# Early adaLN vectors as TensorE products beside the weight slabs, filter parameters inside the first FFN, and layer norm sums accumulated ahead of TensorE

## The chip, the cores and the metric

The kernel runs on one core of one Trainium2 chip. The metric is the device time of one execution in microseconds. A core has a matrix engine (TensorE, PE in the profile, with its weight loads as PEld), three other engines that compute (VectorE as DVE, ScalarE as ACT, GpSimd as POOL), and SyncE (SP), which here only starts transfers. Each engine works through its own list of instructions in order. Transfers run on 16 DMA engines, through queues; an instruction on SP, or on POOL, puts a transfer into a queue.

## The reference

Two layers of a decoder trunk work on 512 tokens of 1024 features, all in float32. In both layers each sub-layer is an RMS norm whose result is scaled and shifted by vectors from a conditioning vector c, then a mixer, then an addition that a gate vector from c scales. Layer 0 has a Mamba-2 mixer and a dilated attention mixer in parallel, layer 1 a convolution module with a layer norm; each layer ends with a SwiGLU FFN.

```python
cs = jax.nn.silu(c)
mod = cs @ ada_w[i] + ada_b[i]               # [1024] @ [1024, 6144]
sh1, sc1, g1, sh2, sc2, g2 = split(mod, 6)   # 1024 values each
h = rms_norm(x, norm_mix_g[i]) * (1 + sc1) + sh1
x = x + g1 * mix
h = rms_norm(x, norm_ffn_g[i]) * (1 + sc2) + sh2
x = x + g2 * swiglu(h, wg, wu, wd)
```

The product for mod is the adaLN work. The 6144 values of a layer are 48 columns of 128: columns 0 to 7 are sh1, 8 to 15 sc1, 16 to 23 g1, 24 to 31 sh2, 32 to 39 sc2, 40 to 47 g2. The first two are wanted at the start, g1 with the first output chunk of the mixer, the others only in the FFN. The convolution module computes

```python
u = a * sigmoid(gt)                           # from h @ w1 + b1
u = causal_depthwise_conv(u, w_dw, b_dw)      # 31 taps per feature
mu = mean(u); var = mean((u - mu) ** 2)       # layer norm over 1024 features
u = silu((u - mu) * rsqrt(var + eps) * ln_g + ln_b)
out = u @ w2 + b2
```

## The kernel before

Activations lie with features on the 128 partitions and the 512 tokens along the row: a tensor of 1024 features is 8 tiles of 128 x 512. A large product is float32 made of three products of a faster type: weights and activations are split into a high and a low part, and high x high, low x high and high x low are summed (`products`, lines 221, 222 and 224). A weight slab (`slab`) is 1 MB: it is loaded by SP into a buffer with the tag `raw`, of which the pool `wpool` has two, then ACT casts the high part in two halves (L208) and DVE subtracts for the low part (L209). TensorE writes its results into banks of PSUM, which have tags too: `pj`, `A`, `B` and `C`, with two banks each. Whatever wants a bank or a buffer of a tag waits until an earlier user has been read.

The program is written in the order of the stages below; a planner, which reckons with the time of each instruction, puts them into the list of each engine, the earlier written ones first where several could go. `issue_after` holds an instruction back until a named one.

1. Start (to about 44 us): adaLN columns 0 to 15 with `ada_wide` (eight multiply-adds per 4 columns on DVE, then four transposes on PE and a sum on DVE), the first norm, and the time steps dt of the SSM.
2. SSM (to about 345 us): four groups. `ssm_inputs(g)` makes ten outputs from five slabs: B and C of the group (`bc`), four tiles `x`, four tiles `z`. `ssm_group(g)` goes through four chunks of 128 tokens: `ar` is loaded from DRAM, ACT does relu and exp (L507, L508), PE does `px`, `pb`, `pd`, `po` and `pst`, the last two carrying the state from chunk to chunk; `pst` is in bank C. In the program `ssm_group(g)` stands ahead of `ssm_inputs(g + 1)`, and behind groups 0 and 1 stands `ada_rows` for columns 16 to 19 and 20 to 23: eight loads of 256 KB on SP into three buffers of their own, a matmul for each with silu(c) as a weight of 32 columns (`cs32`, of which only the first isn't zero), the four column tiles of PE in turn, then four sums over the partitions as matmuls with one column (`adac`, L176). Results are in bank C.
3. Attention (345 to about 800 us): for each of eight pairs of heads `att_pair` (scores, exp, three transposes `pt` into bank C for each of two heads, weights of the branches sent through DRAM as `w_dram`, and the results `at`, `ath`, `atl`), then `ada_some`, then `att_inputs` of the next pair (slabs `wa`, `wb`, and `wv` in every second). `ada_some` does three `ada_pool` jobs: a load of 512 KB on POOL's queue into one buffer, four POOL instructions (L184, L186), a PE transpose in bank C (L153) and a sum on DVE, for one column each; the eight calls make columns 24 to 47. Output chunks stand behind some pairs (`y_chunk`, `mixed_chunk`); the last, `mixed_chunk(3)`, is done in two halves of tokens, with the sums of the next norm (`Norm` n1) in it.
4. Parameters of layer 1: `rows` loads vectors as rows and transposes them. The 31 taps become `taps`, then 16 DVE copies make `wcol` (L921), and `filters(0)` to `filters(3)` make the convolution weights on POOL (L930).
5. FFN of layer 0 (to about 1255 us): `Norm.finish` (L285 to L325), slabs, products. `side` is called behind each of its gate and up slabs and does the layer 1 adaLN columns with `ada_wide`, four at a time.
6. Convolution module (to about 1490 us): `conv(k, cols)` for eight tiles k, each in one or two halves of the tokens; `layer_norm(c)` for each half; `pw2`. In `layer_norm` the mean comes from eight matmuls with a constant weight of 1/1024 (`mu`, L1011), DVE subtracts it, ACT squares, and the variance comes from 16 matmuls with one column (`var`, L1021). A float32 matmul of this kind is two instructions in the profile.
7. FFN of layer 1, the last norm, the output.

Of the kernel before, what the change touches and what calls it, by code (L numbers as in the profile page):

```python
# [9 lines left out]
F32 = mybir.dt.float32  # L10
# [3 lines left out]
ALU = mybir.AluOpType  # L14
# [63 lines left out]
def trunk_kernel(ctx: ExitStack, tc, a, out, dbg=None):  # L78
# [86 lines left out]
    def ada_rows(pool, l, j0):  # L165

        ps = bank("C", f"adar{l}_{j0}")
        for k in range(KT):
            w = pool.tile([P, 512], F32, tag="adaw", name=f"adaw{l}_{j0}_{k}", bufs=3)
            nc.sync.dma_start(w, a["ada_w"][l][k * P:(k + 1) * P, j0 * P:j0 * P + 512])  # L170
            PE.matmul(ps[k % 4 * 32:(k % 4 + 1) * 32, :], cs32[:, k, :], w, start=k < 4, stop=k >= 4)
# [3 lines left out]
        for j in range(4):  # L175
            PE.matmul(pm[:, j:j + 1], rw[:, j * P:(j + 1) * P], ones[:, 0:1], start=True, stop=True)  # L176
        V.tensor_tensor(mod[l][:, j0:j0 + 4], pm, adab[l][:, j0:j0 + 4], op=ALU.add)

    def ada_pool(pool, bufs, l, j):
        w = pool.tile([P, 1024], F32, tag="adaw", name=f"adap{l}_{j}", bufs=bufs)  # L180
        G.dma_start(w.rearrange("p (k c) -> p k c", k=KT),
                          a["ada_w"][l][:, j * P:(j + 1) * P].rearrange("(k p) c -> p k c", p=P))
        w3 = w.rearrange("p (k c) -> p k c", k=KT)
        G.tensor_tensor(w3, w3, cs.unsqueeze(2).broadcast_to([P, KT, P]), op=ALU.mult)  # L184
        for n in (512, 256, 128):
            G.tensor_tensor(w[:, 0:n], w[:, 0:n], w[:, n:2 * n], op=ALU.add)  # L186
        ada_finish(l, w, j, 1)

    def ada_jobs(l, lo, hi):
        return [(l, j) for j in range(lo, hi)]  # L190
# [299 lines left out]
    cs32 = ssm.tile([P, KT, 32], F32, name="cs32", bufs=1)  # L490
# [66 lines left out]
    jobs = [(0, j) for j in range(24, 48)]  # L557

    def ada_some(pool, bufs, n):
        for _ in range(min(n, len(jobs))):  # L560
            ada_pool(pool, bufs, *jobs.pop(0))

# [348 lines left out]
    taps = const.tile([P, 31 * KT], F32, name="taps")  # L911
    rows([(dwr[0:128], 128)], "dw0", taps[:, 0:128])
    rows([(dwr[128:248], 120)], "dw1", taps[:, 128:248])

    wcol = const.tile([P, KT, 4, 8], F32, name="wcol")
    V.memset(wcol[96:128, :, :, 7], 0.0)
    taps3 = taps.rearrange("p (t k) -> p k t", k=KT)
    for sft in range(4):
        for g in range(4):
            o = wcol[sft * 32:(sft + 1) * 32, :, g, 0:8 if sft < 3 else 7]  # L920
            V.tensor_copy(o, taps3[g * 32:(g + 1) * 32, :, sft:TAPS:4])  # L921
# [4 lines left out]
    w4 = {}  # L926

# [5 lines left out]
    for k in range(4):  # L933
        filters(k)
# [22 lines left out]
    with tc.tile_pool(name="conf", bufs=2) as conf:  # L957
        h = nxt.finish(const, g_mix1, mod[1][:, 0:8], XG)
        w1 = a["cv_w_pw1"][0]
        cv, u4 = {}, {}  # L960
# [8 lines left out]
        def conv(k, cols):  # L969
# [36 lines left out]
        def layer_norm(c):  # L1006
# [3 lines left out]
            for i, k in enumerate(range(KT)):  # L1010
                PE.matmul(mb, meanw, cv[k, n], start=i == 0, stop=i == KT - 1)  # L1011
            vp = bank("C", f"var{n}", (P, nb))
            for i, k in enumerate(range(KT)):
                t = cv[k, n]
                V.tensor_tensor(t, t, mb, op=ALU.subtract)
                if i % 2 == 0:
                    two = tmp.tile([P, T], F32, tag="st_sq", name=f"cvq{k}_{n}")
                sq = two[:, i % 2 * w:(i % 2 + 1) * w]
                S.activation(sq, t, AF.Square)
                for b in range(nb):  # L1020
                    PE.matmul(vp[:, b:b + 1], sq[:, b * P:(b + 1) * P], ones[:, 0:1], start=i == 0 and b == 0,  # L1021
                              stop=i == KT - 1 and b == nb - 1)
# [86 lines left out]
```

## Time and profile before

| what | value |
|---|---|
| time, median of 3 runs | 1847.52 us (1847.27 to 1849.47) |
| the profiled execution | 1844.22 us, of which the span is 1842.5 us |
| PE busy | 1764.2 us, 96% of the span |
| DVE, ACT, POOL busy | 999.3, 740.7, 347.6 us |
| bytes moved | 247.85 MB, mean 135 GB/s |

The span is the time from the first to the last recorded instruction; the profiled execution's time is 1.7 us more. A row of the timeline gives the start, the time it took, the engine, the line of the program, the operation, the tile that it writes and those it reads, and in square brackets how long its engine had been idle and what it waited for; "x4" means that so many like instructions stand in the row. A row of waits names who waited, for whom, the total, how many times, and the longest. Busy times of PE are modelled for the ends of matmuls, which are pipelined, so neighbours overlap and the time from one start to the next is what counts. PEclk is the clock that the throttle granted to TensorE, as a share of full speed.

### The profile page before, as it was taken

What the parts mean: (1) busy time and instruction counts of PE and PEld (TensorE: products, weight loads), DVE (VectorE), ACT (ScalarE), POOL (GpSimd) and SP (SyncE); (2) the same over time, 40 slices, a digit from 0 to 9 for tenths busy, and PEclk for the clock granted to TensorE, in tenths of its full rate; (3) what the DMA queues carried; (4) which work ended last, traced back from release to release, by engine and by line L of the source; (5) the groups of instructions that cost most, each with busy time, mean ns of one, the idle gap of its engine ahead of it and who ended that gap; (6) DMA issues with size and microseconds to landing.
All of it is one profiled execution on the core that took longest, in us unless ns stands there. A gap on an engine that the chain in (4) does not pass through costs nothing.

```text
span 1842.5 us, 25006 instructions
## 1 busy us (share of the span) xinstructions
PE 1764.2 (96%) x9775; PEld 1438.8 (78%) x9775; DVE 999.3 (54%) x1944; ACT 740.7 (40%) x1473; POOL 347.6 (19%) x278
## 2 busy tenths in 40 slices
PE   5999999999999999977999999999999999999998
PEld 3777687788778787767888888897568988888887
DVE  7756657555655556658674673373204743333336
ACT  6465646455454444434222222252215532122235
POOL 0013314224542423432000000021121100000001
PEclk9999999999999999988999999999998999999999
DMA  9455544454545445343655562253640522323233
GB/s 309 125 143 152 154 119 125 111 150 138 133 131 149 127 157 142 104 128 115 228 187 179 183 206 81 87 177 78 178 122 24 161 92 92 92 92 114 70 97 132
DMA packets 233219, 247.85 MB, mean 135 GB/s; under 512 B 14074, under 2 KB 198204, under 8 KB 233101
## 3 DMA queue, kind: packets, MB, share of 16 engines
q1 hardware_dynamic: 223117, 208.50, 38.0%
q0 software_dynamic: 9984, 37.75, 6.2%
q8 instruction: 77, 1.26, 0.3%
q14 instruction: 41, 0.34, 0.1%
HBM read 228.73 MB, written 8.64 MB: 129 GB/s over the span
## 4 chain that ended last, share of the span: by engine, by line
PE 83%; DVE 6%; DMA 5%; ACT 2%; issue 1%; POOL 1%; SPq 0%; DVEq 0%; ACTq 0%; POOLq 0%
PE fd L221 4%; PE fd L222 4%; PE fd L224 4%; PE fg L222 4%; PE fu L221 4%; PE fg L221 4%; PE fu L222 4%; PE fu L224 4%; PE fg L224 4%; PE cps L975 3%; PE s L733 2%; DMA ar<-a_dram 2%; PE z L221 2%; PE z L222 2%; PE z L224 2%; PE qq L221 2%
## 5 line engine op out<-in xcount | busy, mean ns | idle before, releaser
L221 PE MATMUL fd<-uh,wd_h 128*128 128x512 f32 (+1 forms) x448 | 148.6, 347 | 0.9 <-DVE xT L608 0.9
L222 PE MATMUL fd<-uh,wd_l 128*128 128x512 f32 (+1 forms) x448 | 147.0, 344 | 0.0
L209 DVE TENSOR_TENSOR wf_l<-wf_w,wf_h 128x1024 fp32r<-128x1024 f32 x88 | 106.1, 1241 | 75.4 <-ACT wf_h L208 75.4
L208 ACT CAST wf_h<-wf_w 128x1024 fp32r<-128x1024 f32 x88 | 87.6, 1047 | 116.7 <-PE fd L224 71.9
L263 POOL TENSOR_TENSOR n_acc<-n_acc,n_q 128x256 f32<-128x256 f32 x32 | 30.2, 943 | 526.4 <-ACT n_q L259 526.3
L222 PE MATMUL fg<-n_h,wf_l 128*128 128x512 f32 x320 | 125.3, 391 | 1.0 <-DVE wf_l L209 1.0
L221 PE MATMUL fg<-n_h,wf_h 128*128 128x512 f32 x320 | 125.3, 392 | 0.5 <-ACT wf_h L208 0.5
L222 PE MATMUL fu<-n_h,wf_l 128*128 128x512 f32 x320 | 124.7, 390 | 0.0
L221 PE MATMUL fu<-n_h,wf_h 128*128 128x512 f32 x320 | 124.5, 389 | 0.0
L208 ACT CAST wd_h<-wd_w 128x1024 fp32r<-128x1024 f32 (+1 forms) x64 | 57.1, 940 | 101.3 <-PE fd L224 81.1
L759 ACT ACTIVATE s<-s,nm 128x128 f32<-128x128 f32 x192 | 79.5, 416 | 43.9 <-DVE nm L755 39.9
L885 DVE TENSOR_TENSOR fs<-fs,fu 128x512 f32<-128x512 f32 x40 | 27.5, 688 | 127.3 <-PE fu L224 127.3
L221 PEld LDWEIGHTS fd<-uh,wd_h 128*128 128x128 f32 x448 | 84.1, 188 | 11.9 <-DVE xT L608 1.3
L608 DVE SCALAR_TENSOR_TENSOR xT<-fd,mod,xT 128x512 f32<-128x512 f32 (+1 forms) x64 | 39.1, 615 | 98.3 <-PE fd L224 98.1
L222 PEld LDWEIGHTS fd<-uh,wd_l 128*128 128x128 f32 x448 | 84.2, 188 | 10.5
L224 PE MATMUL fd<-ul,wd_h 128*128 128x512 f32 (+1 forms) x448 | 91.9, 343 | 0.0
L209 DVE TENSOR_TENSOR wd_l<-wd_w,wd_h 128x1024 fp32r<-128x1024 f32 (+1 forms) x64 | 68.2, 1099 | 34.9 <-ACT wd_h L208 34.6
L162 DVE SCALAR_TENSOR_TENSOR adaa<-adaw,cs,adaa 128x512 f32<-128x512 f32 x112 | 85.0, 759 | 2.6
L884 ACT ACTIVATE fs<-fg 128x512 f32<-128x512 f32 x40 | 23.9, 598 | 146.7 <-PE fg L224 146.7
L224 PEld LDWEIGHTS fd<-ul,wd_h 128*128 128x128 f32 x448 | 72.9, 188 | 10.6
L186 POOL TENSOR_TENSOR adap<-adap 128x512 f32<-128x512 f32 (+2 forms) x72 | 79.1, 1099 | 5.0
L224 PE MATMUL fu<-n_l,wf_h 128*128 128x512 f32 x320 | 79.1, 389 | 0.0
(405 smaller groups left out, 4538.9 us busy)
## 6 DMA issues: line engine op xcount, KB each, us to landing
adaw<-in_ada_w POOLq DMA_DIRECT2D x24, 1024.0 KB, 5.7
wf_w<-in_ffn_w_gate SPq DMA_DIRECT2D x22, 1024.0 KB, 5.3
wf_w<-in_ffn_w_up SPq DMA_DIRECT2D x22, 1024.0 KB
wd_w<-in_ffn_w_down SPq DMA_DIRECT2D x16, 1024.0 KB, 5.2
adap<-in_ada_w POOLq DMA_DIRECT2D x24, 512.0 KB, 5.8
wd_w<-in_ffn_w_down SPq DMA_DIRECT2D x16, 768.0 KB, 4.3
wa_w<-in_hy_w_out SPq DMA_DIRECT2D x20, 512.0 KB, 6.8
u<-cu SPq DMA_DIRECT2D x128, 67.5 KB, 2.0
```

What stands on the lines that cost most here:

```text
L162: V.scalar_tensor_tensor(acc, ws[k // 4][:, k % 4, :], cs[:, k:k + 1], acc, op0=ALU.mult, op1=ALU.add)
L186: G.tensor_tensor(w[:, 0:n], w[:, 0:n], w[:, n:2 * n], op=ALU.add)
L208: S.copy(hi[:, s:e], raw[:, s:e])
L209: eng.tensor_tensor(lo[:, s:e], raw[:, s:e], hi[:, s:e].bitcast(F32), op=ALU.subtract)
L221: PE.matmul(ps[:, cols], hi[:, o(k):o(k) + P], xh, start=k == 0, stop=False)
L222: PE.matmul(ps[:, cols], lo[:, o(k):o(k) + P], xh, start=False, stop=False)
L224: PE.matmul(ps[:, cols], hi[:, o(k):o(k) + P], acts[k][1][:, cols], start=False, stop=k == nk - 1)
L263: (V if k >= self.n - 3 else G).tensor_tensor(self.acc, self.acc, sq, op=ALU.add)
L608: V.scalar_tensor_tensor(xT[m][:, cols], ps[:, cols], mod[l][:, go + m:go + m + 1], xT[m][:, cols], op0=ALU.mult, op1=ALU.add)
L733: marks[hp, 0] = marks[hp, 1] = PE.matmul(ps[:, o:o + 2 * wd].rearrange("p (e w) -> p e w", e=2), q, k, start=True, stop=True)
L759: S.activation(s[:, o:o + wd], s[:, o:o + wd], AF.Exp, bias=nm, accum_out=l)
L975: PE.matmul(ps[g * 32:(g + 1) * 32, :], w4[k][:, g * 8 + m, :], u4[k][:, g, t:t + w], start=m == 0, stop=m == 7)
```

## The change

There are three parts.

`ada_pool` and `ada_some` are gone. `ada_rows` now loads its 2 MB as two slabs of 1 MB with SP into the `raw` buffers of `wpool`, does eight matmuls (the four column tiles for the four blocks of a slab), copies the result to SBUF and returns a function `fin`, which holds the four sums and the DVE add. It is called behind `ssm_group(g)` for three groups (columns 16, 20 and 24 onward), with `fin` behind the next group's inputs, and ahead of `att_pair(hp)` for the first five pairs (28 to 44 onward), with `fin` behind the next pair's inputs. `cs32` moves to a pool that lives through the attention.

`conv_params` holds the loads and transposes of the taps, the copies to `wcol`, and `filters(0)` to `filters(3)`. It is called by the third `side()` in the first FFN, and all but the filters is held back until the norm's last instruction.

In the convolution module a sum `csum` of the first seven tiles is kept as they come (k = 1 to 4 on POOL, 5 and 6 on DVE), so that the mean takes two matmuls for each half; the squares are kept in pairs, DVE adds three of the four pairs, and the variance takes eight single-column matmuls for each half.

```diff
     def ada_rows(pool, l, j0):
         ps = bank("C", f"adar{l}_{j0}")
-        for k in range(KT):
-            w = pool.tile([P, 512], F32, tag="adaw", name=f"adaw{l}_{j0}_{k}", bufs=3)
-            nc.sync.dma_start(w, a["ada_w"][l][k * P:(k + 1) * P, j0 * P:j0 * P + 512])
-            PE.matmul(ps[k % 4 * 32:(k % 4 + 1) * 32, :], cs32[:, k, :], w, start=k < 4, stop=k >= 4)
+        for i in range(2):
+            w = pool.tile([P, 2048], F32, tag="raw" if pool is wpool else "adaw", name=f"adaw{l}_{j0}_{i}", bufs=2 if pool is wpool else 1)
+            w = w.rearrange("p (k c) -> p k c", k=4)
+            nc.sync.dma_start(w, a["ada_w"][l][i * 512:(i + 1) * 512, j0 * P:j0 * P + 512].rearrange("(k p) c -> p k c", p=P))
+            for k in range(4):
+                PE.matmul(ps[k * 32:(k + 1) * 32, :], cs32[:, 4 * i + k, :], w[:, k, :], start=i == 0, stop=i == 1)
         rw = tmp.tile([P, 512], F32, tag="st_sq", name=f"adas{l}_{j0}")
         S.copy(rw, ps)
-        pm = bank("C", f"adac{l}_{j0}", (P, 4))
-        ...
+        def fin():
+            pm = bank("C", f"adac{l}_{j0}", (P, 4))
+            ...
+        return fin
-    def ada_pool(pool, bufs, l, j):
-        ...
-    cs32 = ssm.tile([P, KT, 32], F32, name="cs32", bufs=1)
+    cs32 = early.tile([P, KT, 32], F32, name="cs32", bufs=1)
     for g in range(GROUPS):
         ssm_group(g, *ins)
-        if g < 2:
-            ada_rows(ssm, 0, 16 + 4 * g)
+        if g < 3:
+            fin = ada_rows(wpool, 0, 16 + 4 * g)
         if g + 1 < GROUPS:
             ins = ssm_inputs(g + 1)
+            fin()
     for hp in range(8):
+        fin = ada_rows(wpool, 0, 28 + 4 * hp) if hp < 5 else None
         acts.append(att_pair(hp, r, vps))
-        ada_some(att, 1, 3)
         if hp < 7:
             r, vps = att_inputs(hp + 1, vps)
+        if fin:
+            fin()
-    rows([(dwr[0:128], 128)], "dw0", taps[:, 0:128])
-    ...
+    def conv_params():
+        with tc.issue_after(nrm.tail.ins):
+            rows([(dwr[0:128], 128)], "dw0", taps[:, 0:128])
+            rows([(dwr[128:248], 120)], "dw1", taps[:, 128:248])
+            V.memset(wcol[96:128, :, :, 7], 0.0)
+            ...
+        for k in range(4):
+            filters(k)
         def side():
             ...
+                    if len(wides) == 10:
+                        conv_params()
         def conv(k, cols):
             ...
+                if k == 1:
+                    csum[c.start] = conf.tile([P, T // 2], F32, tag=f"csum{c.start}", name=f"csum{c.start}", bufs=1)
+                    G.tensor_tensor(csum[c.start], cv[0, c.start], o, op=ALU.add)
+                elif 1 < k < KT - 1:
+                    (G if k < 5 else V).tensor_tensor(csum[c.start], csum[c.start], o, op=ALU.add)
         def layer_norm(c):
-            for i, k in enumerate(range(KT)):
-                PE.matmul(mb, meanw, cv[k, n], start=i == 0, stop=i == KT - 1)
+            PE.matmul(mb, meanw, csum[n], start=True, stop=False)
+            PE.matmul(mb, meanw, cv[KT - 1, n], start=False, stop=True)
             ...
+                if k % 2 == 0:
+                    two = conf.tile([P, T], F32, tag="cvq", name=f"cvq{k}_{n}", bufs=3)
+                S.activation(two[:, k % 2 * w:(k % 2 + 1) * w], t, AF.Square)
+                if k == 1:
+                    vacc = two
+                elif k in (3, 5):
+                    V.tensor_tensor(vacc, vacc, two, op=ALU.add)
+            for i, sq in enumerate((vacc, two)):
+                for b in range(2 * nb):
+                    PE.matmul(vp[:, b % nb:b % nb + 1], sq[:, b * P:(b + 1) * P], ones[:, 0:1], start=i == 0 and b == 0,
+                              stop=i == 1 and b == 2 * nb - 1)
```

More of the change, by code (lines that the diff above doesn't have):

```diff
@@ L167, in ada_rows @@
         ps = bank("C", f"adar{l}_{j0}")
[L168 to L171 removed]
+        for i in range(2):
[4 more added lines that the diff above has]
+                PE.matmul(ps[k * 32:(k + 1) * 32, :], cs32[:, 4 * i + k, :], w[:, k, :], start=i == 0, stop=i == 1)
         rw = tmp.tile([P, 512], F32, tag="st_sq", name=f"adas{l}_{j0}")
         S.copy(rw, ps)
[L174 to L190 removed]
+        def fin():
+            pm = bank("C", f"adac{l}_{j0}", (P, 4))
+            for j in range(4):
+                PE.matmul(pm[:, j:j + 1], rw[:, j * P:(j + 1) * P], ones[:, 0:1], start=True, stop=True)
+            V.tensor_tensor(mod[l][:, j0:j0 + 4], pm, adab[l][:, j0:j0 + 4], op=ALU.add)
+        return fin
     SL = (G, V, V, V)
@@ L555, in ssm_group @@
         nc.sync.dma_start(yd_dram[4 * g:4 * g + 4].rearrange("t p l -> p t l"), y1)
[L557 to L561, printed above, removed]
     ins = ssm_inputs(0)
@@ L926, in trunk_kernel @@
     w4 = {}
+    taps = const.tile([P, 31 * KT], F32, name="taps")
+    wcol = const.tile([P, KT, 4, 8], F32, name="wcol")
+    def conv_params():
[3 more added lines that the diff above has]
+            V.memset(wcol[96:128, :, :, 7], 0.0)
+            taps3 = taps.rearrange("p (t k) -> p k t", k=KT)
+            for sft in range(4):
+                for g in range(4):
+                    o = wcol[sft * 32:(sft + 1) * 32, :, g, 0:8 if sft < 3 else 7]
+                    V.tensor_copy(o, taps3[g * 32:(g + 1) * 32, :, sft:TAPS:4])
+        for k in range(4):
+            filters(k)
     def filters(k):
@@ L959, in trunk_kernel @@
         w1 = a["cv_w_pw1"][0]
-        cv, u4 = {}, {}
+        cv, u4, csum = {}, {}, {}
         def shifted(k, u):
@@ L1009, in layer_norm @@
             mb = bank("A", f"mu{n}", (P, w))
-            for i, k in enumerate(range(KT)):
-                PE.matmul(mb, meanw, cv[k, n], start=i == 0, stop=i == KT - 1)
+            PE.matmul(mb, meanw, csum[n], start=True, stop=False)
+            PE.matmul(mb, meanw, cv[KT - 1, n], start=False, stop=True)
             vp = bank("C", f"var{n}", (P, nb))
-            for i, k in enumerate(range(KT)):
+            vacc = None
+            for k in range(KT):
                 t = cv[k, n]
                 V.tensor_tensor(t, t, mb, op=ALU.subtract)
[L1016 to L1022, printed above, removed]
+                if k % 2 == 0:
[9 more added lines that the diff above has]
+                              stop=i == 1 and b == 2 * nb - 1)
             vv = tmp.tile([P, nb], F32, tag="st_v", name=f"lnv{n}")
```

11 lines of the change are left out of this document (removed).

## The prediction, made before the changed kernel was run

> **What bounds the kernel now.** I read the page first, then the waits of PE, then busy time by stage.
>
> ```profile
> span 1842.5 us, 25006 instructions
> PE 1764.2 (96%) x9775; PEld 1438.8 (78%) x9775; DVE 999.3 (54%) x1944; ACT 740.7 (40%) x1473; POOL 347.6 (19%) x278
> ```
> ```profile
> PE ada L153 <- POOL adap L186: 10.2, 2, 7.7
> PE x L221 <- DVE sc L460: 6.5, 3, 2.3
> PE n_b L288 <- DVE n_d L285: 4.4, 2, 4.0
> PE f_a L221 <- ACT n_h L322: 4.1, 2, 3.4
> PE wa L221 <- DVE xT L608: 3.5, 4, 1.9
> ```
> ```profile
> 106.20:183.60 77.40, 75.36 (x387) 57.21 (x387) 47.69 (x60) 41.95 (x79) 21.80 (x15) 0.98 0.53 148
> 345.00:798.00 453.00, 446.25 (x2443) 359.48 (x2439) 264.59 (x771) 211.07 (x592) 164.31 (x132) 1.00 0.46 132
> 798.00:856.30 58.30, 36.73 (x230) 34.15 (x230) 42.66 (x79) 20.35 (x35) 28.55 (x24) 0.80 0.43 125
> 856.30:1255.00 398.70, 396.87 (x2083) 340.82 (x2084) 239.89 (x390) 129.56 (x198) 37.13 (x38) 1.00 0.49 160
> ```
> The last four rows are stretches: length, then busy time of PE, weight loads, DVE, ACT and POOL, then the granted clock, the DMA share and GB/s. TensorE sets the end. It idles 2.04 us in one SSM group (106 to 184 us) and 6.75 us in all the attention pairs up to 798 us. One stretch is bad: the last output chunk and the norm (798 to 856 us) have 21.6 us of idle PE, and the granted clock is 0.80. So taking adaLN work off POOL is worth something in that stretch only; everywhere else the change is paid in PE time.
>
> **Gain 1: the tail of attention.** Two waits of 10.2 us are put down to the pool job. The longer one is only partly its own:
>
> ```profile
> 616.68 1.24 SPq L804 DMA_DIRECT2D at<-w_dram  x2
> 799.22 1.24 SPq L804 DMA_DIRECT2D at<-w_dram  x2
> ```
> ```profile
> 622.58 1.29 DVE L821 TENSOR_TENSOR at<-o,at 128x512 f32<-128x512 f32 x2 [4.34 <-DMA at<-w_dram]
> 807.78 1.29 DVE L821 TENSOR_TENSOR at<-o,at 128x512 f32<-128x512 f32 x2 [3.00 <-DMA at<-w_dram]
> 810.79 0.98 DVE L827 TENSOR_TENSOR atl<-at,ath 128x512 fp32r<-128x512 f32 x1 [0.68 <-ACT ath L826]
> 833.90 4.46 DVE L921 COPY wcol<-taps 32x64 f32<-32x64 f32 x16
> 847.62 3.77 DVE L285 TENSOR_SCALAR n_d<-cst,n_y 128x128 f32<-128x128 f32 x2
> 1393.06 0.48 DVE L285 TENSOR_SCALAR lnr_d<-cst,ln_y 128x128 f32<-128x128 f32 x2
> ```
> ```profile
> 845.66 7.51 POOL L930 TENSOR_TENSOR w<-id,wcol 128x1024 f32<-128x1024 f32 x4 [2.24 <-PE wa L224]
> ```
> The pair's own chain (weights of the last pair back from DRAM, then at, ath, atl) ends at 811.77, eight microseconds after the wait began. In pair 4 at arrives 5.90 us after its issue (616.68 to 622.58), here 8.56, beside the pool job's load and sums: of the 7.7 us I take 3.5 back (2.7 of landing, 0.8 of at, ath and atl behind). The second ada wait (10.2 - 7.7 = 2.5) gives 2.0; what follows is again the weight slab. The 16 copies of wcol hold DVE 4.46 us in the middle of the residuals; with them go the 1.9 us wait on xT and a half-clock piece behind it: 3.6. Then the norm: n_d takes 3.77 us beside the POOL filters and 0.48 in the same form without (3.3), and the later slices behind it take less; I take 7.3 with the 4.1 us wait for n_h, which shortens by about 3.
>
> Half clock follows the waits, for 3.5 us each, and costs half of that (the first row follows a wait for sc, the second that for ada):
>
> ```profile
> 139.50:143.00 3.50, 3.50 (x10) 2.72 (x9) 3.46 (x6) 3.47 (x11) 1.17 (x1) 0.51 0.57 151
> 825.60:829.10 3.50, 3.50 (x17) 3.50 (x18) 1.61 (x6) 0.73 (x2) 0.59 (x1) 0.51 0.73 244
> ```
> The piece at 825.6 goes (1.7). A longer one over the norm's end, which with these makes the 0.80 of the stretch, I shorten by 0.9. Sum 3.5 + 2.0 + 3.6 + 7.3 + 1.7 + 0.9 = 19. Bounds: 8 if the at chain and DVE's queue keep the end where it is and only the wcol, ada and half-clock terms come (2.0 + 3.6 + 1.7 and 0.7 of n_d), 24 if the whole 21.6 of idle and a little clock go.
>
> **Gain 2: a late slab at 765 us.**
>
> ```profile
> 764.63 2.68 DVE L209 TENSOR_TENSOR wy_l<-wy_w,wy_h 128x1024 fp32r<-128x1024 f32 x1
> 768.15 1.19 PE L733 MATMUL s<-kz,q 128*128 128x256 f32 x2 [2.62 <-DVE m L736]
> ```
> Half of this slab was split on DVE beside a pool job's sums and held the maxima m behind it for 2.68 us; PE waited 2.62 us. With half of a half-clock piece behind it (0.9) I take 3.5; bounds 0, if the slab comes as late without POOL, and 4.3 with the whole piece.
>
> **Gain 3: layer norm sums.**
>
> ```profile
> 1371.57 1.93 PE mu L1011 x8
> 1383.79 1.88 PE var L1021 x16
> ```
> An fp32 product is two instructions here, so 32 instructions make the mean over both halves and 64 the variance. 24 of the 32 go; 8 in 1.93 us are 0.24 each, most runs nearer 0.225: 5.4. Of the variance 32 go at 1.88 / 16 = 0.117: 3.7. Sum 9. POOL and DVE take the adds of csum, DVE those of the squares; POOL's trail the convolutions, which PE needs anyway. Without that cover, the two DVE adds of a half come ahead of the mean, with about 3 us a half: the low bound is 3, the high one 9.5.
>
> Gains: 19 + 3.5 + 9 = 31.5.
>
> **Cost 1: the products themselves.**
>
> ```profile
> 126.67 1.06 PE L171 MATMUL adar<-adaw,cs 128*32 128x512 f32 x6
> 127.66 0.50 PE L224 MATMUL bc<-n_l,wbc_h 128*128 128x512 f32 x1
> L153 PE MATMUL ada<-cst,adap x24: 270/272/476, 420.0 to 825.6; 128*128 128x128 f32 x24
> ```
> Six instructions (three column tiles, two passes) fill PE 0.99 us. Four tiles cost hardly more: 1.05 per half slab, 2.1 per group, and 0.9 for the single-column sums: 3.0. Eight groups are 24. The two old groups cost 10.8 (two triples of 1.1 and two singles of 1.15 each, 4.5, and 0.9), the 24 transposes 24 x 0.12 = 2.9. Net +10.3, bounds 7 (a half slab in 0.85) and 14 (0.23, one more pass, on each of 16 halves). ACT copies each result once more (about 0.6 us, six groups); it is 40% busy and nothing waits for it but the late sums.
>
> **Cost 2: the SSM groups.** Old ada tiles had buffers of their own; new ones take both raw buffers, which every weight slab needs, and SP's queue.
>
> ```profile
> 107.26 0.38 SPq L505 DMA_DIRECT2D ar<-a_dram  x1
> 47.94 1.36 SPq L170 DMA_DIRECT2D adaw<-in_ada_w  x3
> ```
> ```profile
> 117.91 4.85 DMA ar<-a_dram
> 122.79 2.46 ACT ar L507 x8
> 886.39 1.81 PE fg L224 x8
> ```
> ```profile
> wf_w<-in_ffn_w_gate SPq DMA_DIRECT2D x22, 1024.0 KB, 5.3
> ```
> ```profile
> 108.67 0.48 PE L221 MATMUL bc<-n_h,wbc_h 128*128 128x512 f32 x1
> 125.50 1.02 PE L544 MATMUL pst<-xde,btok 128*128 128x512 f32 x2
> 447.80 0.27 PE L153 MATMUL ada<-cst,adap 128*128 128x128 f32 x1
> 447.91 0.60 PE L772 MATMUL pt<-cst,s 128*128 128x128 f32 x4
> ```
> The adaw tiles were issued at 47.94, yet adar ran only at 126.67, right behind the chunk's pst (125.50), long after bc of the next group had begun (108.67). Likewise pt of a pair comes 0.11 us behind the third ada transpose. So I read bank C as handed out in program order: adar cannot run before the last pst of the group. Until then its slab holds the raw buffers, and wbc, wanted as filler from 108.67 on, is queued behind it on SP. A product of 512 columns is 1.81 / 8 = 0.226 us; bc has 48 of them, 10.8 us of filler. Without it, the third chunk's ar is issued at 107.26, lands 4.85 later, takes 2.46 for relu and some 2.3 for exp and the product with cb: 116.9. Then pst at 117, the first half of adar to 118, the wbc slab 5.3 and its cast about 1.2: bc at 124.6. In the 18.5 us from 106.1 PE has about 14 to do: of the group's 75.36 busy us ten outputs take 54 and the old adar 5.4, so 16 are the four chunks', three quarters of them here (12), and 2.1 for adar. That leaves 4.5 idle, in three groups 13.5, and a half-clock loss of 1.7 in two of them, 3.4. Against it, the waits for sc go (6.5, with two half-clock losses 3.4: 9.9), since bc then comes with its x slabs waiting. Net +7. Bounds: -10 if filler is found, +37.5 if the whole of bc (10.8 us of PE) and 1.7 of clock is lost three times.
>
> By the Trainium skill, "TensorE: Matmul & The Clock Gate", section "What's actually happening", the clock halves only after an idle window of some 3.4 us; no trace here agrees, since no wait for sc was over 2.3 and that for ada at 825.6 was 2.5, and both rows behind them stand at 0.51. By that rule the new pieces of idle would cost no clock, and the sum would be 3.4 us less; I go by the rows.
>
> **Cost 3: heads of the attention pairs.** ada_rows now stands before att_pair, so its two loads are ahead of the pair's bias and of the next wa slab in SP's queue, its bank C turn ahead of pt. Ten loads of 1 MB enter SP's queue in the attention, while 24 of 512 KB leave POOL's. For the first pair adar also follows the spread of ry in bank C. I take +3, about one short wait of 0.6 a pair; zero if all slabs come early, 26 if each of five pairs loses 5.3, one slab's load. The sums of single columns and their DVE add stand behind the next pair's inputs and hold nothing.
>
> **Cost 4: FFN 0.** The wcol copies (4.46) and filters (7.51) now run there, the copies on DVE ahead of the third wide job, the two loads of the taps on SP behind the norm's last instruction; PE is 99.5% busy there and DVE 60%. +0.5, bounds 0 and 3.
>
> Costs: 10.3 + 7 + 3 + 0.5 = 20.8. **Sum** 20.8 - 31.5 = -10.7. The profiled execution took 1844.22 us (span 1842.5 and 1.7 around it), 3.3 under the median of 1847.52: 1833.5 on its scale, 1837 as a median.
>
> **Rivals.** Slower: the filler is starved. Each of three SSM groups loses all of bc's cover, 3 x 10.8 = 32.4 with nothing given back, instead of +7: 1837 + 25 = 1862. It decides from the point where costs 2 and 3 pass 31.5 - 10.8 = 20.7. For it: the shared raw buffers and bank C's order; against it: pd, po and pst of other chunks may fill. No starvation: the planner finds a place for adar early, or reads slabs before them, and costs 2 and 3 are nothing: 1827. For it: PE idles only 2 us in a group now. Gains fail: the tail keeps its end by the at chain (8, not 19) and the mean waits for the adds (3, not 9): 1837 + 17 = 1854, or 1848 with the first alone; it is the change not doing what it says.
>
> **Chances.** Forecast 0.44, starved 0.24, no starvation 0.20, gains fail 0.12. 0.2% is 3.7 us, about what a measurement of this kernel tells from no change. Faster: all of no starvation, 0.38 of the forecast's 0.44 and 0.01 of the failed gains, 0.59. Same: 0.04 of the forecast and 0.05 of failed gains, 0.03 of starved ones, 0.12. Slower: the rest, 0.29. The range 1819 to 1861 reaches from the good ends of the SSM cost (-10) and the tail to starvation; the forecast's own is 1828 to 1846.
>
> **What would show it.** Right: ada off the waits, the stretch from att pair 7 to the first gate product at about 39 us, n_d at 0.5 us; mu with 8 instructions; the wait for sc replaced by PE waits before bc, about 4.5 us in each of three groups, with the slab's cast as releaser. Wrong: bc still running at 108 us beside the chunk chain (then 1827), or waits over 8 us per group (1862); the wait for n_h still near 4; a wait of pt or wa behind adar in the five pairs; wy or wa slabs late without POOL's sums.

## The result, and the profile after

The changed kernel is slower: a median of 1858.32 us (1856.75 to 1860.34) against 1847.78 for the kernel before beside it, a ratio of 1.0055 (95% interval 1.0031 to 1.0079). The two profiled executions are 1860.34 and 1844.22 us, their spans 16.1 us apart; stages are compared in these two. By the medians the kernel is 10.5 us slower, not 16.1. Other profiled executions of one kernel lay up to 15 us from its median, so that a verdict here rests on a ratio, and a profile tells where time goes inside an execution.

Two lines of the page of the changed kernel, then four of its waits of PE (total, times, longest). Two others of that size, which lie mostly at the start, the kernel before has too.

```profile
span 1858.6 us, 24986 instructions
PE 1767.1 (95%) x9839; PEld 1437.8 (77%) x9839; DVE 963.3 (52%) x1910; ACT 743.8 (40%) x1479; POOL 204.4 (11%) x166
```
```profile
PE pst L537 <- ACT btok L533: 13.7, 6, 4.5
PE bc L214 <- ACT wbc_h L201: 7.7, 3, 2.9
PE wa L214 <- ACT ath L814: 5.6, 1, 5.6
PE pq L214 <- ACT ch L1035: 4.9, 1, 4.9
```

POOL lost 143 us of work and PE gained 3, and the wait for POOL is gone. In its place stand waits in the SSM, for `btok` and for `wbc_h`, of which the kernel before had 0.5 us. The two fences that follow hold the same four stages of the kernel before and of the changed one (SSM behind the first group's inputs, attention to the last pair, tail, first FFN), with the columns named in the prediction. The tail begins with the scores of the last pair, at 760.63 and 800.64.

```profile
105.78:336.25 230.47, 223.03 (x1154) 170.96 (x1152) 144.31 (x181) 126.59 (x237) 67.51 (x46) 0.99 0.50 136
336.25:760.63 424.38, 420.46 (x2312) 340.32 (x2311) 249.55 (x696) 199.31 (x545) 159.56 (x128) 1.00 0.49 139
760.63:856.31 95.68, 71.27 (x406) 60.38 (x405) 63.43 (x161) 37.19 (x94) 36.33 (x30) 0.86 0.35 105
856.31:1229.82 373.51, 372.71 (x1889) 317.36 (x1889) 222.89 (x338) 115.14 (x168) 23.66 (x30) 1.00 0.50 165
```
```profile
107.17:358.60 251.43, 228.27 (x1181) 177.94 (x1180) 146.43 (x185) 129.03 (x239) 64.77 (x47) 0.95 0.49 140
358.60:800.64 442.04, 433.74 (x2406) 344.03 (x2405) 211.56 (x658) 201.51 (x550) 26.59 (x21) 1.00 0.44 132
800.64:876.51 75.87, 65.62 (x402) 55.37 (x400) 47.42 (x136) 37.14 (x94) 11.78 (x12) 0.93 0.34 108
876.51:1253.86 377.35, 373.41 (x1892) 317.28 (x1892) 232.59 (x357) 114.99 (x168) 33.10 (x34) 1.00 0.49 164
```

The SSM costs 21.0 us more (15.7 of them idle PE: 7.4 became 23.2), the attention 17.7, the first FFN 3.8; the tail gives back 19.8. With 1.4 more ahead of these stages and 7.9 less behind them (convolution module and second FFN) that makes 16.1. Other profiles here hold one stage or the other unchanged, and show how sharp such a difference is. In seven profiles with the SSM's adaLN as before, the SSM takes 228.7 to 234.2 us, in four with the changed one 249.4 to 252.7. The attention takes 422.7 to 430.0 us in four profiles with its old code and 440.8 to 444.6 in seven with the new.

This is the first group of the SSM in the changed kernel: the timeline of SP, then of PE, then of ACT, then two stretches behind its two waits.

```profile
75.93 0.37 SPq L171 DMA_DIRECT2D adaw<-in_ada_w  x1
87.75 0.37 SPq L171 DMA_DIRECT2D adaw<-in_ada_w  x1
122.68 0.38 SPq L193 DMA_DIRECT2D wbc_w<-in_hy_w_in  x1
```
```profile
118.77 2.04 PE L537 MATMUL pst<-xde,btok 128*128 128x512 f32 x2 [3.77 <-ACT btok L533]
120.61 0.63 PE L509 MATMUL pb<-sc,sb 128*128 128x128 f32 x2
121.17 2.29 PE L173 MATMUL adar<-adaw,cs 128*32 128x512 f32 x16
...
129.38 0.80 PE L214 MATMUL bc<-n_h,wbc_h 128*128 128x512 f32 x1 [2.77 <-ACT wbc_h L201]
```
```profile
114.57 2.44 ACT L500 ACTIVATE ar<-ar,acs 128x128 f32<-128x128 f32 x8 [3.69 <-DMA ar<-a_dram]
...
118.39 0.24 ACT L533 COPY btok<-pb 128x128 f32<-128x128 f32 x1
```
```profile
118.80:122.30 3.50, 3.50 (x12) 1.44 (x16) 1.88 (x4) 3.39 (x9) 0.00 (x0) 0.55 0.00 0
...
129.40:132.80 3.40, 3.40 (x13) 3.11 (x14) 3.40 (x4) 1.05 (x1) 0.00 (x0) 0.59 1.14 327
```

The two ada slabs are issued at 75.93 and 87.75, and are read only at 121.17, right behind the third pst. Only then does SP issue wbc, and bc begins at 129.38, 22 us behind the last z; before, it was 3 us (105.78 to 108.67). Both waits are followed by a stretch at about half the clock. Over the stage there are six such pieces, 27.2 us in all at a granted clock of 0.50, where the kernel before has two with 6.8 us.

### The profile page after: what moved, and what is told of

Its sections match the earlier page's. It is cut to its first block, busy times and chain, and to the rows that moved or that the text cites. A ratio compares the mean times of both kernels' runs of the same rounds, so it can differ in the third digit from the quotient of the medians.

```text
span 1858.6 us, 24986 instructions
## 1 busy us (share of the span) xinstructions
PE 1767.1 (95%) x9839; PEld 1437.8 (77%) x9839; DVE 963.3 (52%) x1910; ACT 743.8 (40%) x1479; POOL 204.4 (11%) x166
## 4 chain that ended last, share of the span: by engine, by line
PE 83%; DMA 7%; DVE 5%; ACT 4%; issue 1%; SPq 1%; POOL 0%; DVEq 0%; ACTq 0%; POOLq 0%
PE fd L214 4%; PE fd L215 4%; PE fd L217 4%; PE fg L215 4%; PE fu L214 4%; PE fu L215 4%; PE fu L217 4%; PE fg L217 4%; PE fg L214 4%; PE cps L970 3%; PE x L214 2%; PE z L214 2%; PE z L215 2%; PE x L217 2%; PE x L215 2%; PE z L217 2%
## 5 line engine op out<-in xcount | busy, mean ns | idle before, releaser
L215 PEld LDWEIGHTS fd<-uh,wd_l 128*128 128x128 f32 x448 | 84.2, 188 | 10.5
L162 DVE SCALAR_TENSOR_TENSOR adaa<-adaw,cs,adaa 128x512 f32<-128x512 f32 x112 | 89.4, 799 | 2.6
L217 PE MATMUL fg<-n_l,wf_h 128*128 128x512 f32 x320 | 79.0, 389 | 0.0
```

Source lines behind the costliest of these rows:

```text
L162: V.scalar_tensor_tensor(acc, ws[k // 4][:, k % 4, :], cs[:, k:k + 1], acc, op0=ALU.mult, op1=ALU.add)
L215: PE.matmul(ps[:, cols], lo[:, o(k):o(k) + P], xh, start=False, stop=False)
L217: PE.matmul(ps[:, cols], hi[:, o(k):o(k) + P], acts[k][1][:, cols], start=False, stop=k == nk - 1)
```

## The experiments

Ratios are to the kernel before on the same chip, with their 95% interval. Stage times are from each run's profile.

**The SSM: who holds bc up?** Four edits on the changed kernel. The first gives the slabs buffers of their own.

```diff
-            fin = ada_rows(wpool, 0, 16 + 4 * g)
+            fin = ada_small(ssm, 0, 16 + 4 * g)   # eight tiles [P, 512], tag "adaw", bufs=3
```


> The changed kernel, but the three SSM groups load their adaLN weights in eight tiles of 256 KB into three buffers of their own (as the kernel before did for two groups), with the column sums still behind the next group's inputs. Bank C and the place in the program stay. Theory (the ada slabs hold both raw buffers until the third pst, so bc has no slab): bc starts again about 3 us behind the last z of the group, the PE waits for btok and for bc's cast (21 us with the half clock behind them) go, and the time is 1837 to 1842. Rival (the place in the program and bank C hold bc up whatever the buffers): bc still starts 22 us behind z, 1856 to 1860.

Measured: 1845.52 us, 0.9992 (0.9974 to 1.0010). bc starts at 109.75, 2.9 us behind z, in the same place of the program and with the same bank, and the waits for btok and bc are gone. The start of bc, and the SSM as a stretch:

```profile
109.75 0.48 PE L233 MATMUL bc<-n_h,wbc_h 128*128 128x512 f32 x1
```
```profile
106.87:343.59 236.72, 228.68 (x1182) 172.84 (x1180) 144.04 (x183) 126.45 (x238) 65.99 (x47) 0.99 0.51 141
```

The stage is 6.3 us over the kernel before, which has one group of products fewer. The theory's mechanism holds; the time is 3.5 us above its range, since the stage gives back 14.7 us of the 21 that it reckoned with.

The second writes the products behind the next inputs.

```diff
-        if g < 3:
-            fin = ada_rows(wpool, 0, 16 + 4 * g)
         if g + 1 < GROUPS:
             ins = ssm_inputs(g + 1)
-            fin()
+            ada_rows(wpool, 0, 16 + 4 * g)()
```


> The changed kernel, but in the SSM ada_rows with its two 1 MB slabs in the raw buffers is written behind the next group's inputs instead of ahead of them. Theory: wbc gets its buffer as before, the ada slabs come with the z slabs, and the three groups cost little more than their products on PE (3 us each): 1837 to 1842. Rival (any ada slab in the raw buffers starves the stage, wherever it stands): 1850 to 1860, with PE waits before z or in the chunk chain instead of before bc.

Measured: 1843.22 us, 0.9971 (0.9956 to 0.9986). With the 1 MB slabs in the raw buffers, but behind wz, bc again starts 2.9 us behind z, and the SSM takes 226.8 us, less than in the kernel before:

```profile
106.79:333.60 226.81, 219.76 (x1149) 167.49 (x1148) 145.18 (x177) 124.06 (x235) 68.67 (x45) 1.00 0.52 146
```

The rival is out; the time is 1.2 us above the theory's range. So it is what is queued behind the slabs, not the kind of slab.

The third moves adar out of bank C.

```diff
-            fin = ada_rows(wpool, 0, 16 + 4 * g)
+            fin = ada_rows(wpool, 0, 16 + 4 * g, "pj")   # tag of the bank
```


> The changed kernel, but the adar product of the three SSM groups is written into a bank of the tag pj, which the chunk chain does not use, instead of bank C. Slabs, buffers and place in the program stay. Theory (adar waits for its turn in bank C behind the third pst, and its slabs with it): adar runs right behind the last z, the wbc load starts about 12 us earlier, bc starts at about 10 us behind z instead of 22, and half of the SSM loss comes back: 1844 to 1850. Rival (bank C has no part in it): adar stays behind the third pst, 1856 to 1860.

Measured: 1885.99 us, 1.0208 (1.0186 to 1.0229). From its timeline of PE, and from its waits:

```profile
110.03 1.92 PE L173 MATMUL adar<-adaw,cs 128*32 128x512 f32 x16
...
120.08 0.78 PE L214 MATMUL bc<-n_h,wbc_h 128*128 128x512 f32 x1
```
```profile
PE x L214 <- DVE sc L453: 18.6, 3, 6.7
PE pd L516 <- DVE ar L512: 13.0, 3, 4.9
```

Here the mechanism and the time part ways. adar runs 11 us earlier, right behind z as the theory said, and bc starts 13 us behind z (it said about 10), so the turn in bank C is what the slabs had waited for. Yet the time rises beyond both ranges: x now waits 6 us a group for sc, and pd 4 for ar. In the trace of the first group the slabs that come early stand ahead of the chunks on ACT: the casts of wbc and wx run from 118.61 to 125.52, and the relu of the last chunk's ar begins behind them at 125.55, where it began at 118.68 in the changed kernel. No run changes that order alone, so that this is a reading and not shown.

A fourth edit gives the copy of btok, the wait named in the profile, to another engine.

```diff
-                S.copy(btok, pb[:, P:2 * P])
+                V.tensor_copy(btok, pb[:, P:2 * P])
```


> The changed kernel, but the copy of btok from PSUM is done by DVE instead of ACT, where it stood behind relu and exp of the next chunk. Theory (of the SSM loss, the 3.8 to 4.5 us waits of pst for btok in three groups, each with a half-clock piece behind it, are a term of their own, which comes on top of the held slabs): the waits for btok go, the third pst and so bc come 3 to 4 us earlier in each group, and 10 to 15 us come back: 1844 to 1850. Rival (the buffers alone set the date of bc, and the wait for btok is only where the idle time shows): the idle time moves to pd or bc and the time stays at 1855 to 1860.

Measured: 1866.45 us, 1.0093 (1.0067 to 1.0119). The rival's mechanism holds, though the time is 6 us above its range: the wait is now "pd for ar", 13.1 us in all, and bc starts 25 us behind z. btok had only been the last thing in ACT's queue behind relu and exp of a late ar.

**The parts.** Each part of the change by itself, and the change without its adaLN part.

```diff
-        if g < 3:
-            fin = ada_rows(wpool, 0, 16 + 4 * g)
+        if g < 2:
+            ada_rows(ssm, 0, 16 + 4 * g)          # as before
...
-        fin = ada_rows(wpool, 0, 28 + 4 * hp) if hp < 5 else None
         acts.append(att_pair(hp, r, vps))
+        ada_some(att, 1, 3)                       # as before
```


> The changed kernel with the adaLN part as it was before (two groups of small products in the SSM, 24 jobs on POOL in the attention); the parameters inside the first FFN and the layer norm sums as changed. Theory, by stages of the two traces: the convolution module and what follows keep their 7 to 8 us, the tail keeps its waits for the POOL jobs (10 us) but loses the wcol copies and the slow n_d (about 10), the first FFN costs 3 to 4: 1832 to 1838. Rival (the tail's 20 us came from the ada part alone): 1841 to 1845.

Measured: 1836.75 us, 0.9920 (0.9886 to 0.9953). The theory holds. The adaLN part thus costs 1.35% (1.0055 less 0.9920), some 25 us, and the other two gain 0.8%. The tail fell from 95.7 to 80.9 us though its waits for POOL stayed (6.0 and 2.5).

For the layer norm alone, the hunks of `conv` and `layer_norm` are put into the kernel before.

> The kernel before with the layer norm part alone (sums accumulated as the tiles come, squares in pairs). By the stages of the traces of before and changed, from the first mean product to the end it saves 7 to 8 us, against the 9 of the prediction, since a new wait of 4.9 us for the first ch stands where 0.7 stood: ratio to the kernel before 0.9955 to 0.9965. Rival (the sums only move to DVE and POOL): 0.9985 to 1.000.

Measured: 1842.88 us, 0.9942 (0.9921 to 0.9963). From the first mean product to the end of the span it takes 466.8 us instead of 472.6. The rival is out; the ratio is better than the theory's range, while the stages show a little less than it said, 5.7 us.

For the parameters alone, the hunk of `conv_params` and its call are put into the kernel before.

> The kernel before with the move of the taps, wcol and filters(0) to filters(3) into the first FFN alone. By the stages (no_ada_change against before) the tail from the seventh pair on gets 10 to 14 us shorter and the first FFN 2.6 us longer: ratio 0.993 to 0.996. Rival (the tail is set by the at chain and the POOL jobs, so the copies and filters were hidden): 0.998 to 1.001.

Measured: 1844.26 us, 0.9969 (0.9948 to 0.9990). The tail takes 83.4 us instead of 95.7, the first FFN 376.1 instead of 373.5. The stages are as the theory said; the ratio lies between the two ranges.

**The attention.** First the five groups are left out.

```diff
-        fin = ada_rows(wpool, 0, 28 + 4 * hp) if hp < 5 else None
+        fin = ada_rows(wpool, 0, 28 + 4 * hp) if hp < 0 else None
...
+    V.memset(mod[0][:, 28:48], 0.0)
```


> The changed kernel without the five adaLN groups of the attention: columns 28 to 47 are left out and set to zero, so the last adaLN vectors of layer 0 are not computed. It shows what the five groups cost. By products alone (5 x 3.0 us) the time falls by 15 us, to 1843 to 1845; by the stage (442.0 us against 424.4 before, which had 2.9 us of transposes) it falls by 18 to 21, to 1837 to 1840. If the time falls by less than 12, part of the products runs in time that was idle.

Measured: 1835.64 us, 0.9912 (0.9885 to 0.9939). The stretch of its attention:

```profile
358.11:774.89 416.78, 415.38 (x2285) 338.11 (x2284) 210.24 (x653) 198.81 (x545) 26.57 (x21) 1.00 0.41 115
```

The stage falls from 442.0 to 416.8, so five groups cost 25 us, not 15. By the starts of PE's instructions 14.7 are products (10.5 adar, 4.2 adac); idle PE falls from 8.3 to 1.4, and the scores s from 43.0 to 38.7. Why a score takes longer with the groups there is not shown.

Then they are written behind the pair, and next given buffers of their own.

```diff
-        fin = ada_rows(wpool, 0, 28 + 4 * hp) if hp < 5 else None
         acts.append(att_pair(hp, r, vps))
         if hp < 7:
             r, vps = att_inputs(hp + 1, vps)
+        if hp < 5:
+            ada_rows(wpool, 0, 28 + 4 * hp)()
```


> The run that wrote the SSM's ada_rows behind the next inputs (ratio 0.9971), with the five groups of the attention also written behind the pair and the next pair's inputs instead of ahead of the pair. Theory (the five groups cost 25 us in the attention, of which 15 are products and 10 come from standing ahead: slabs before the pair's own in the raw buffers, bank C ahead of the pair's transposes): the attention falls by 5 to 10 us, ratio 0.992 to 0.994. Rival (any group of products with its slabs costs 5 us wherever it stands): the ratio stays at 0.996 to 0.998.

Measured: 1844.14 us, 0.9966 (0.9950 to 0.9982). The rival holds: the stage takes 446.0 us, against 444.6 with the groups ahead. PE's waits for the cast wa slabs, 3.6 us with the groups ahead, fall to 0.2, but waits of the scores for m and at (4.2 us) stand in their place.

```diff
-        fin = ada_rows(wpool, 0, 28 + 4 * hp) if hp < 5 else None
+        fin = ada_small(att, 0, 28 + 4 * hp, 2) if hp < 5 else None   # bufs=2 of [P, 512]
```


> The run with own buffers in the SSM (ratio 0.9992), with the five groups of the attention also loaded in eight tiles of 256 KB each, into two buffers of their own (the buffer wr is single for that, to have room); place in the program and bank C stay. The attention stage took 442.0 us with the five groups and 417.0 without them: 14.7 are products, 6.9 idle, about 4 slower scores. Theory (here too the slabs in the raw buffers keep the pair's own slabs away, so PE idles and scores run without other products between them): idle falls to 2 to 4 us, the scores to 38 to 40 us, the stage to 432 to 436, ratio 0.994 to 0.997. Rival (place and bank C make it): the stage stays at 440 to 444, ratio 0.998 to 1.001.

Measured: 1867.80 us, 1.0102 (1.0061 to 1.0142), outside both. Of this run the stretch of the attention, the group of its adar products (all eight groups: busy time, mean ns), and one product in the timeline:

```profile
343.50:804.33 460.83, 458.47 (x2407) 345.57 (x2406) 213.32 (x658) 201.26 (x550) 26.64 (x21) 1.00 0.44 126
```
```profile
L171 PE MATMUL adar<-adaw,cs 128*32 128x512 f32 x128 | 46.5, 605 | 0.1
```
```profile
402.21 1.04 PE L171 MATMUL adar<-adaw,cs 128*32 128x512 f32 x2
403.18 0.51 PE L233 MATMUL kq<-n_h,wa_h 128*128 128x512 f32 x1
```

Idle falls to 2.4 and the scores to 38.5, near the values without any group, as the theory said. But the products come one at a time, as tiles arrive, and one alone holds PE 0.97 us; they take 31.3 us in this stage instead of 10.5. Buffers, size of the tiles and PE's extra 21 us changed together, and the last by itself gives every slab more time, so that this run doesn't show that the raw buffers alone had made the idle time.

**The tail and POOL.** Here the POOL jobs are kept, four behind each of the first six pairs.

```diff
-        ada_some(att, 1, 3)
+        ada_some(att, 1, 4)                       # on the run without the adaLN change
```


> The parameters inside the first FFN and the layer norm sums as changed, the SSM's adaLN as before, and the POOL jobs of the attention as before but four behind each of the first six pairs instead of three behind each of eight, so that none falls in the last output chunk. Against the same kernel with three jobs a pair (ratio 0.992 to the kernel before) the two waits for POOL (6.0 and 2.5 us) and the half clock behind them go, while the wait for ath keeps some 5: 4 to 8 us less, ratio 0.988 to 0.990. Rival (four jobs a pair make POOL and DVE late in the short pairs): 0.992 to 0.996, with new PE waits for ada or pt before 660 us.

Measured: 1859.68 us, 1.0042 (1.0020 to 1.0063). It is slower than both ranges, the rival's way but with another wait than it named, here in its waits of PE and in its timeline of DVE:

```profile
PE s L733 <- DVE at L821: 12.0, 2, 6.4
```
```profile
482.21 1.29 DVE L821 TENSOR_TENSOR at<-o,at 128x512 f32<-128x512 f32 x2 [5.68 <-DMA at<-w_dram]
```

The planner's order changed: at, waiting for its load, now stands on DVE ahead of the maxima that the next scores need, at 482 and again at 605 us.

Next, fewer jobs instead of denser ones: columns 40 to 47, the gates of the FFN, go to DVE in that FFN.

```diff
-    jobs = [(0, j) for j in range(24, 48)]
+    jobs = [(0, j) for j in range(24, 40)]
-        wides = [(1, j) for j in range(0, 48, 4)]
+        wides = [(0, 40), (0, 44)] + [(1, j) for j in range(0, 48, 4)]
-            for _ in range(2 if len(wides) == 2 else 1):
+            for _ in range(2 if len(wides) in (6, 4, 2) else 1):
```


> The parameters inside the first FFN and the layer norm sums as changed, the SSM's adaLN as before, 16 POOL jobs (columns 24 to 39) in the attention, three behind a pair, so that they end with the sixth pair, and columns 40 to 47, which are first used at the first residual of the FFN, made on DVE by the first two calls of side (the parameters of the convolution move two calls further, the layer 1 columns double up at the end). Theory: no wait for POOL is left in the last output chunk and no group of products in the attention; against the run without the adaLN change (0.992) 5 to 9 us less in the tail and 2 to 5 us less in the attention, 2 us more in the FFN: ratio 0.986 to 0.990, faster than all others. Rival (the FFN's DVE, now with two more jobs, or a shifted order in the attention takes it back): 0.992 to 0.996.

Measured: 1826.98 us, 0.9874 (0.9835 to 0.9912): faster than both kernels, whose ratios lie outside its interval. From the run without the adaLN change (0.9920) it is not told apart, as their intervals overlap. The tail takes 74.9 us, the first FFN 376.0, the attention 426.9 (not less than before).

Last, the two groups of the SSM are made on DVE; their sum then stands behind the next group's inputs.

```diff
-            PE.matmul(ps[k % 4 * 32:(k % 4 + 1) * 32, :], cs32[:, k, :], w, start=k < 4, stop=k >= 4)
+            V.scalar_tensor_tensor(acc, w, cs[:, k:k + 1], acc, op0=ALU.mult, op1=ALU.add)   # k = 0: multiply
...
```


> The run late_gate_columns (0.9874), with the two groups of the SSM (columns 16 to 23) made by multiply-adds on DVE, as at the start, instead of products with one column on PE. The old two groups take 10.8 us of PE, the new ones four transposes each, about 1 us in all; DVE, 62% busy in the stage, gets 12 us more. Theory (PE time is the price in the SSM too): 6 to 10 us less, ratio 0.982 to 0.984. Rival (DVE's products for the chunk chain come late behind them): 0.986 to 0.990, with longer waits for DVE in the SSM.

Measured: 1829.38 us, 0.9896 (0.9865 to 0.9927). The rival holds. In the SSM PE is busy for 9.6 us less and idle for 8.5 us more, waiting for DVE, once 6.6 us for cb; ahead of it, the first group's inputs take 5.3 us longer.

**The first FFN.** The first edit calls the filters one per side call.

```diff
-        for k in range(4):
-            filters(k)
...
+                    if 5 <= len(wides) <= 8:
+                        filters(8 - len(wides))
```


> The changed kernel, but filters(0) to filters(3) are made by four successive calls of side, one each, instead of all in the third. Theory (the first FFN costs 3.8 us more because four filters in a row on POOL slow the multiply-adds of the wide job on DVE, 7.7 us for four, and PE waits 1.8 us for its result): that wait goes, the first FFN takes 375 to 376 us instead of 377.4. Rival (the 16 copies of wcol are what makes DVE late): 377 to 378.

Measured: one run, 1862.14 us, first FFN 377.3. The edit moved nothing: the planner still put all four in a row on POOL, so that theory and rival stay open. The second edit queues them behind the loads of a wide job.

```diff
+                        with tc.issue_after(marks['ada'].ins):
+                            filters(8 - len(wides))
```


> The changed kernel, but each of filters(0) to filters(3) is queued on POOL behind the loads of a later wide job, so that they no longer run in a row. In the changed kernel four multiply-adds of the wide job took 7.7 us beside them (3.0 at 0.75 each) and PE then waited 1.8 us. Theory (POOL's filters slow DVE): the four take 3 to 5 us, the wait of 1.8 us goes, the first FFN takes 374.5 to 376 us instead of 377.4. Rival (the wcol copies ahead of them on DVE make it late): the multiply-adds take 3 us but PE still waits over 1 us.

Measured: one run, 1855.45 us, first FFN 373.63 us, as before the change and 0.9 us below the theory's range. The timeline of DVE, POOL and PE of the changed kernel, then of this one:

```profile
936.72 7.71 DVE L162 SCALAR_TENSOR_TENSOR adaa<-adaw,cs,adaa 128x512 f32<-128x512 f32 x4
...
936.77 9.44 POOL L925 TENSOR_TENSOR w<-id,wcol 128x1024 f32<-128x1024 f32 x4 [2.74 <-DVE wcol L919]
...
944.49 0.44 PE L153 MATMUL ada<-cst,adaa 128*128 128x128 f32 x2 [1.80 <-DVE adaa L162]
```
```profile
932.82 3.12 DVE L162 SCALAR_TENSOR_TENSOR adaa<-adaw,cs,adaa 128x512 f32<-128x512 f32 x4
...
937.00 1.93 POOL L923 TENSOR_TENSOR w<-id,wcol 128x1024 f32<-128x1024 f32 x1
```

Four multiply-adds take 7.71 us beside the filters and 3.12 without, with the wcol copies ahead of them in both. The Trainium skill, "GPSIMD Engine Reference", section "1. Specifications", says that GpSimd shares its SBUF interfaces with VectorE, with contention for VectorE's instructions that read two inputs from SBUF. The multiply-adds read two (adaw and adaa), and these rows agree.

The same two lines were then put into the run late_gate_columns.

> The run late_gate_columns (0.9874) with each of filters(0) to filters(3) queued on POOL behind the loads of a later wide job, as in the run filters_held. Theory (the two effects are in different stages and add): the first FFN falls from 376.0 to about 373.6 us, ratio 0.985 to 0.987. Rival (the two further wide jobs already make DVE the limit there): the first FFN stays at 376, ratio 0.987 to 0.990.

Measured: 1823.29 us, 0.9875 (0.9836 to 0.9914). The first FFN took 377.4 us in its profile, not 373.6: the two gains don't add, and this version is no faster than late_gate_columns. In late_gate_columns PE has no wait for adaa in the first FFN, so the wait that the held filters took away was no longer there.

## Why the prediction was wrong

It forecast 1837 us, faster than before; the kernel came out slower, near the slower rival (1862) and by its mechanism. That it lies so near is in part luck: that rival reckoned 32.4 us for the SSM, which cost 22.8, and the rest came from other stages. By the prediction's own terms:

- **Cost 2, the SSM, is the step that failed:** +7 with the products' -1.8, so 5.2, against 21.0. The mechanism (slabs that hold both raw buffers behind bank C's turn, with wbc queued behind) was right, and own buffers and the other place undo it. The size was wrong, in idle time and in clock. Idle time was to rise by 7.0 (13.5 less the 6.5 for sc) and rose by 15.7. bc came at 129.4, not 124.6: 1.4 of that since the stage began later, the rest because ar landed late, adar and pst ran at half clock, and wbc was issued at 122.68 and not near 118. So the two waits of a group were 6.5 to 6.9, not 4.5 (3.77 and 2.77 in the first). Busy time was to fall by the products' 1.8 and rose by 5.2: each group had two half-clock pieces (0.55 and 0.59 in the first), two of them 6.8 us long, where I had counted two pieces in all and set them off against two that went. By the Trainium skill, "TensorE: Matmul & The Clock Gate", section "What's actually happening", the clock is halved after an idle window of about 3.4 us. The first wait, of 3.77 us, agrees with that; the second, of 2.77 us, was followed by 0.59 all the same, so the rows were the better guide again.
- **Cost 1, the products:** 15 us for five groups, measured 14.7. Right.
- **Cost 3, heads of the pairs:** +3. The attention rose 17.7, and products less the old transposes are 13.0 of that (14.7 less 1.7), which leaves 4.7; by the means of the profiles named above it rose 16 and leaves 3. The short waits were there (3.6 us for the cast wa slabs, none before), so this term was about right. Against no group at all 10 us are left beside the products, idle time and longer scores; what makes them up was not separated.
- **Cost 4, the first FFN:** +0.5, measured +3.8. I had used the POOL filters' slowing of DVE as a gain in the norm (n_d 3.77 to 0.48, now 0.55) and not asked what they would slow in their new place.
- **Gains 1 and 2, the tail:** both lie in this stage, the slab at 765 us too, so -22.5, measured -19.8. The parameters alone bring 12.3 of it. The wait for the last pair stayed at 5.6, a fall of 2.1 where 3.5 was forecast; that of the scores for m fell from 2.8 to 1.4, where 2.6 was to go.
- **Gain 3, layer norm:** -9, measured -7.4 from the first mean product on in the changed kernel and -5.7 alone. PE's products fell as counted, but the first pw2 product now waits 4.9 us for ch where it waited 0.7: the chain behind the sums had been covered by them.

Of the 27 us between the forecast change (-10.7) and the profiled one (+16.1) the SSM makes 16, the first FFN, the tail and the attention about 3 each, and the start and the layer norm the rest. The slower rival was to decide from 20.7 us for costs 2 and 3; cost 2 alone measured 22.8 (21.0 and the 1.8 of products saved).

## What to carry to other kernels

A load that is moved into shared buffers must be costed by when it is *read*, not by its bytes: if its reader waits for a turn elsewhere, everything queued for the same buffers waits too, and here the engine with the cover removed paid twice, in idle time and in clock. A moved interference (here POOL beside DVE) is a gain in one place and a price in the next. And a wait that the profile names can be only the last of a queue: moving the named copy to another engine moved the wait.

## What was not expected of the hardware

One product with a 32-column weight holds PE 0.97 us when it stands alone between other products (402.21 to 403.18), while eight of them in a row, four column tiles at a time, took 1.92 us (16 instructions at 110.03). And work on POOL cost PE less than I had thought: with 21 POOL jobs the attention took 422.7 to 430.0 us in four profiles, with none 416.8, so 6 to 13 us for 21 columns, where the products of 20 columns cost 25.
